# Group A's output squares on GpSimd with one VectorE sum, and group B's outputs scaled for two heads in one operation

## The chip, the cores and the metric

The kernel runs on 1 core of one Trainium2 chip. The metric is the device time of one execution in microseconds. The core has five engines that each work through a queue of instructions in order and wait for one another by semaphores: TensorE (PE in the profile, its weight loads PEld), VectorE (DVE), ScalarE (ACT), GpSimd (POOL) and SyncE (SP), which here issues the DMAs.

## The reference

Two layers of an encoder over 1024 tokens of width 1024, all in float32. What matters here is the attention of the two head groups and what is done to their outputs:

```python
for l in range(DEPTH):                                   # 2 layers
    proj = rms_norm(x, pre_norm_g[l]) @ w_in[l]
    aq, ak, av, ag, bq, bk, bv, bg = jnp.split(proj, SPLIT_POINTS, axis=-1)
    # group A: 4 heads of 128 columns, two softmaxes p[0] - lam * p[1] with a position bias
    oa = diff_attention(aq, ak, av, lam, rel_bias)
    oa = rms_norm(oa, diff_subln_g[l]) * (1.0 - lam_init)       # per head, over its 128 columns
    ya = oa.reshape(bn, s_len, A_WIDTH) * jax.nn.silu(ag)
    # group B: 8 query heads of 64 columns on 2 key heads, q and k normalised and rotated
    ob = gqa_attention(q, k, bv)
    yb = ob * jax.nn.silu(bg)
    y = jnp.concatenate([ya, yb], axis=-1) @ w_out[l]
    x = x + rms_norm(y, post_norm_g[l])
```

`rms_norm(x, g)` is `x * rsqrt(mean(x * x) + 1e-6) * g`. So each row of each of group A's heads needs the sum of 128 squares, and each row of group B's heads needs a division by its softmax sum.

## The kernel before, in words

Tokens are in 8 tiles of 128. Each layer has three stages: the projections, the attention loop, and the output projection. In profiles of this kernel almost every instruction has line 67, that of a helper, so one reads it by tile names: `pS`, `pT`, `pO` are PSUM buffers (two each of scores, transposes and outputs), `e` holds probabilities, `w` split weights or split transposed probabilities, `o` an output on its way to its transpose (2 buffers), `y` the rows that the output projection reads, `s` small per-row numbers.

**The loop.** It goes over 4 heads `h` of group A and, within each, 4 groups `g` of two token tiles: 16 steps a layer. A step takes group A's head `h` and the pair `hp` of group B's heads that goes with it, on 256 tokens. It has 8 items: 4 of group A (two softmaxes for each token tile) and 4 of group B (two heads, two tiles). `tick` handles one item: the row maximum on VectorE (for group A the custom operation that adds the bias as well), the next item's scores on TensorE, one part of an output product, the exponential on ScalarE. Later work is put on lists: `after(n, fn, mid)` runs `fn` n ticks on, in the middle of the tick if `mid`, otherwise at its end; `trans` holds the transposes of probabilities, `parts` the parts of the output products. Within the loop each engine keeps the order in which the code names its instructions (`tc.keep_in_program_order`). So the order on the engines is the order of these lists.

**Group A's output.** `a_out` multiplies values and probabilities into `pO` (transposed: columns of the head by tokens), four parts of 6 matmuls. `finish` copies that to an `o` tile, `oT`. `norm` transposes it back on TensorE into the other half of `pO`, `p4`, and squares it. `gate` copies it into the rows `yv`, and GpSimd works out the factor of each row from the sums of squares `ms` and the reciprocal softmax sums `r0` and scales the rows.

**Group B's output.** `b_out` does the same for two heads, whose values are split in a high and a low half that lie side by side. `finish` copies one half to `oT`; `add`, a tick later, adds the other on VectorE and, for the second head, inverts the softmax sums `sr`; `back` transposes on TensorE at the end of that tick; `store`, one tick later, scales into the rows.

**The tail.** After the last item `tick` goes on while lists are not empty, and the code puts four conversions of output weights (`half_convs`) and the first two transposed row tiles (`y_transposed`, which multiplies with the gates and splits on ScalarE, VectorE and GpSimd) between its ticks. Behind it the output projection begins; there, a scheduler orders the instructions.

Of the kernel before, what the change touches and what calls it, by code (L numbers as in the profile page):

```python
# [11 lines left out]
AF = mybir.ActivationFunctionType  # L12
ALU = mybir.AluOpType
AX = mybir.AxisListType
# [3 lines left out]
P = 128  # L18
# [35 lines left out]
def hybrid_encoder(ctx, tc, x, rel_bias, pre_norm_g, w_in, diff_lambda, diff_subln_g,  # L54
# [18 lines left out]
    pe, dve, act, gps = Engine(nc.tensor), Engine(nc.vector), Engine(nc.scalar), Engine(nc.gpsimd)  # L73
# [11 lines left out]
    def nm(p):  # L85
        uid[0] += 1
        return f"{p}{uid[0]}"
# [10 lines left out]
    def y_tile(shape=(P, D), dt=F32):  # L98
        return sb.tile(list(shape), dt, tag="y", name=nm("y"), bufs=8)

    def o_tile(shape=(P, 512), dt=F32):
        return sb.tile(list(shape), dt, tag="o", name=nm("o"), bufs=2)

    def s_tile(n=1, tag="s", bufs=12):
        return sm.tile([P, n], F32, tag=f"{tag}{n}", name=nm("s"), bufs=bufs)
# [7 lines left out]
    def ps_o():  # L113
        return ps.tile([P, 512], F32, tag="O", name=nm("pO"), bufs=2)
# [189 lines left out]
    def layer(l, hT, ends, given):  # L304
# [14 lines left out]
        def row_tile(t):  # L319
            if ys[t] is None:  # L320
                ys[t] = y_tile()
            return ys[t]
# [435 lines left out]
        def after(delay, fn, mid=False):  # L758
            later_q.append((now[0] + delay, mid, fn))
# [96 lines left out]
        def a_out(h, g, aT, r0):  # L856
            box = []

            def part(i):
                if i == 0:  # L860
                    box.append(ps_o())
                pO = box[0][:, 0:256]
                V = values[h]
                for k in (2 * i, 2 * i + 1):
                    pe.matmul(pO, V[:, 0, k, :], aT[0][:, k, :], start=(k == 0), stop=False)
                    pe.matmul(pO, V[:, 0, k, :], aT[1][:, k, :], start=False, stop=False)
                    pe.matmul(pO, V[:, 1, k, :], aT[0][:, k, :], start=False, stop=(k == NK - 1))
                if i == 3:
                    after(0, lambda: finish(box[0]))

            def finish(pO):
                oT = o_tile((P, 256))
                act.copy(oT, pO[:, 0:256])
                p4 = pO[:, 256:512].rearrange("p (q c) -> p q c", c=P)
                ms = s_tile(2, "oms", 3)
                yv = [row_tile(g * 2 + qi)[:, h * P:(h + 1) * P] for qi in range(2)]

                def norm():
                    for qi in range(2):
                        pe.transpose(p4[:, qi, :], oT[:, qi * P:(qi + 1) * P], ident)  # L880
                    for qi in range(2):
                        act.activation(oT[:, :P], p4[:, qi, :], AF.Square, accum_out=ms[:, qi:qi + 1])
                    after(1, gate, True)

                def gate():
                    for qi in range(2):
                        dve.tensor_copy(yv[qi], p4[:, qi, :])
                    fr = s_tile(2, "ofr", 3)
                    gps.tensor_tensor(fr, r0[:, :2], r0[:, :2], ALU.mult)
                    gps.tensor_tensor(ms, ms, fr, ALU.mult)  # L890
                    gps.tensor_scalar(ms, ms, 1.0 / P, EPS, ALU.mult, ALU.add)
                    gps.tensor_tensor(ms, ms, mhalf[:, :2], ALU.pow)
                    gps.tensor_tensor(fr, ms, r0[:, :2], ALU.mult)
                    for qi in range(2):
                        gps.tensor_scalar(yv[qi], yv[qi], fr[:, qi:qi + 1], 0.0, ALU.mult, ALU.add)
                after(1, norm)

            return [lambda i=i: part(i) for i in range(4)]
# [27 lines left out]
        def b_out(hp, g, BV, bT, sr):  # L926
            kv = hp // 2
            box, halves = [], []

            def part(j, i):  # L930
                if not halves:
                    halves.append(o_tile((P, 256)))
                if i == 0:
                    box.append(ps_o())
                pO = box[j][:, 0:256]
                for k in range(4 * i, 4 * i + 4):
                    pe.matmul(pO, BV[:, kv, k, :], bT[j][0][:, k, :], start=(k == 0), stop=False)
                    pe.matmul(pO, BV[:, kv, k, :], bT[j][1][:, k, :], start=False, stop=(k == NK - 1))
                if i == 1:
                    after(0, lambda: finish(j, box[j], halves[0]))  # L940

            def finish(j, pO, oT):
                mine = slice(j * 64, j * 64 + 64)
                other = slice(64 - j * 64, 128 - j * 64)
                act.copy(oT[mine], pO[other, 0:256])

                def add():
                    dve.tensor_tensor(oT[mine], oT[mine], pO[mine, 0:256], ALU.add)
                    if j == 1:
                        dve.reciprocal(sr, sr)  # L950
                        after(0, back)
                after(1, add, True)
                p4 = pO[:, 256:512].rearrange("p (q c) -> p q c", c=P)

                def back():
                    for qi in range(2):
                        pe.transpose(p4[:, qi, :], oT[:, qi * P:(qi + 1) * P], ident)
                    after(1, store, True)

                def store():  # L960
                    for qi in range(2):
                        for jj in range(2):
                            c0 = 512 + hp * P + jj * 64
                            dve.tensor_scalar(row_tile(g * 2 + qi)[:, c0:c0 + 64], p4[:, qi, jj * 64:jj * 64 + 64],
                                              sr[:, jj * 2 + qi:jj * 2 + qi + 1], None, ALU.mult)

            return [[lambda j=j, i=i: part(j, i) for i in range(2)] for j in range(2)]

# [277 lines left out]
```

## Time and profile before

| | |
|---|---|
| runs | 1414.98, 1415.23, 1417.01 us; median 1415.23 |
| the profiled execution | 1416.01 us, its span 1414.3 us |
| granted TensorE clock | 0.997 on average |
| busy share of the span | VectorE 73%, ScalarE 59%, GpSimd 51% |
| attention loops with their tails | about 305 to 617 us and 1003 to 1317 us |

The profiled execution's own time is 1.7 us longer than its span, from the first to the last instruction. A row of the timeline gives the start in us from the span's start, the length in us, the engine, the line, the operation, the tiles (out<-in) with their shapes, how many instructions are merged, and in brackets how long the engine had been idle and what ended that.

### The profile page before, as it was taken

The numbers are of one execution on the slowest core, as the hardware profiler recorded it, in microseconds if no ns is written. First come the engines' busy times: TensorE is split into PE (matmuls) and PEld (weight loads), VectorE is DVE, ScalarE is ACT, GpSimd is POOL, SyncE is SP. The second block draws the span as 40 slices with busy tenths as digits, with TensorE's granted clock in tenths as the row PEclk, the third lists the DMA queues.
The fourth block names the chain that finished last, engine by engine and source line by source line (L and its number), as shares of the span: only waits on it lengthen the run. The fifth ranks groups of instructions, "written<-read, shape, count | busy, mean of one in ns | idle before, by whom it ended". The sixth has DMA issues, their size and how long they took to land.

```text
span 1414.3 us, 22659 instructions
## 1 busy us (share of the span) xinstructions
PE 1385.7 (98%) x8108; PEld 1214.0 (86%) x8108; DVE 1033.3 (73%) x1737; ACT 832.1 (59%) x1586; POOL 724.2 (51%) x827
## 2 busy tenths in 40 slices
PE   7999999999999999999999999999999999999998
PEld 6888888889999999978788888888899999999787
DVE  7879854478888888852787797554788888888423
ACT  6323443378888888843442143333888888888321
POOL 5530000068888888874343200001888888888641
PEclk9999999999999999999999999999999999999999
DMA  6456436583514232143524455337823151222313
GB/s 225 125 154 188 161 133 224 165 247 91 126 53 111 68 98 90 46 134 119 180 93 122 128 155 178 119 112 225 217 70 87 53 155 53 71 87 84 125 61 134
DMA packets 134784, 179.12 MB, mean 127 GB/s; under 512 B 10112, under 2 KB 98432, under 8 KB 132368
## 3 DMA queue, kind: packets, MB, share of 16 engines
q1 hardware_dynamic: 134672, 177.67, 41.6%
q8 instruction: 64, 1.05, 0.3%
q14 instruction: 48, 0.39, 0.1%
HBM read 120.98 MB, written 60.85 MB: 129 GB/s over the span
## 4 chain that ended last, share of the span: by engine, by line
PE 91%; POOL 3%; DVE 2%; DMA 2%; ACT 1%; issue 1%; POOLq 0%; DVEq 0%; SPq 0%; ACTq 0%
PE pO L67 38%; PE pS L67 32%; PE pT L67 21%; POOL w L67 1%; DVE y L67 1%; DMA h<-aq_d 1%; POOL e L67 1%; ACT e L67 1%; POOL h L67 0%; DVE w L67 0%; DMA e<-in_pre_norm_g_dram 0%; DVE h L67 0%; DVE s L67 0%; DMA e<-x_d 0%; ACT w L67 0%
## 5 line engine op out<-in xcount | busy, mean ns | idle before, releaser
L67 PE MATMUL pO<-w,h 128*128 128x256 f32 (+1 forms) x3160 | 551.0, 322 | 2.6 <-POOL w L67 2.6
L67 PEld LDWEIGHTS pO<-w,h 128*128 128x128 f32 x3160 | 486.1, 189 | 67.2 <-POOL w L67 3.6
L67 PE MATMUL pS<-h,h 128*128 128x512 f32 x1024 | 293.6, 409 | 0.6 <-DMA h<-aq_d 0.5
L67 POOL TENSOR_TENSOR y<-y,y 128x512 fp32r<-128x512 f32 x12 | 15.5, 1292 | 382.2 <-ACT y L67 192.6
L67 PE MATMUL pT<-identr,e 128*128 128x128 f32 x1536 | 200.5, 273 | 0.5
L67 PEld LDWEIGHTS pS<-h,h 128*128 128x128 f32 x1024 | 174.9, 189 | 24.4 <-ACT w L67 0.7
L67 DVE TENSOR_TENSOR w<-pT,w 128x512 fp32r<-128x512 f32 x256 | 169.9, 685 | 35.4 <-ACT w L67 35.2
L67 PEld LDWEIGHTS pT<-identr,e 128*128 128x128 f32 x1536 | 172.5, 140 | 5.2 <-DVE w L67 4.2
L67 POOL TENSOR_TENSOR w<-e,w 128x512 fp32r<-128x512 f32 x128 | 166.2, 1299 | 10.4
L67 ACT CAST w<-pT 128x512 fp32r<-128x512 f32 x256 | 143.9, 588 | 40.8 <-PE pT L67 38.0
L67 DVE TENSOR_REDUCE s<-pS 128x1 f32<-128x1024 f32 x128 | 156.4, 1222 | 15.0 <-PE pS L67 14.1
L67 DVE CUSTOM_DVE_ANT_0 e<-pS,h 128x1024 f32<-128x1024 f32 x128 | 155.6, 1217 | 6.7 <-PE pS L67 6.1
L67 ACT ACTIVATE e<-e,s 128x1024 f32<-128x1024 f32 x128 | 148.2, 1158 | 19.5 <-DVE s L67 18.8
L67 POOL TENSOR_TENSOR e<-e,e 128x1024 f32<-128x1024 f32 x64 | 153.3, 2395 | 5.3
L67 ACT ACTIVATE e<-pS,s 128x1024 f32<-128x1024 f32 x128 | 144.6, 1130 | 5.6 <-DVE s L67 5.2
L67 PE MATMUL pT<-h,w 128*128 128x512 f32 x528 | 122.5, 389 | 0.0
L67 PE MATMUL pS<-w,h 128*128 128x512 f32 (+1 forms) x576 | 118.0, 362 | 0.0
L67 PEld LDWEIGHTS pT<-h,w 128*128 128x128 f32 x528 | 99.0, 188 | 20.9 <-ACT w L67 0.2
L67 PEld LDWEIGHTS pS<-w,h 128*128 128x128 f32 x576 | 96.6, 194 | 14.6
L67 POOL TENSOR_SCALAR e<-e,s 128x1024 f32<-128x1024 f32 x64 | 72.0, 1126 | 72.0 <-DVE s L67 68.3
L67 ACT ACTIVATE o<-pO 128x128 f32<-128x128 f32 (+3 forms) x101 | 39.4, 390 | 108.6 <-PE pO L67 107.4
L67 POOL TENSOR_TENSOR s<-s,mhalf 128x2 f32<-128x2 f32 (+2 forms) x96 | 80.0, 834 | 8.0
(102 smaller groups left out, 1794.2 us busy)
## 6 DMA issues: line engine op xcount, KB each, us to landing
h<-aq_d SPq DMA_DIRECT2D x64, 256.0 KB, 5.1
h<-in_w_in_dram SPq DMA_DIRECT2D x20, 512.0 KB, 4.7
bq_d<-y SPq DMA_DIRECT2D x64, 128.0 KB, 2.4
av_d<-e SPq DMA_DIRECT2D x32, 256.0 KB, 2.3
e<-in_w_in_dram SPq DMA_DIRECT2D x16, 512.0 KB, 4.7
y<-in_w_in_dram SPq DMA_DIRECT2D x16, 512.0 KB, 6.3
ak_d<-e SPq DMA_DIRECT2D x32, 256.0 KB, 2.0
gate_d<-e SPq DMA_DIRECT2D x32, 256.0 KB, 2.0
```

Of the source, the lines that this page charges most:

```text
L67: ins = fn(*args, **kw)
```

## The change

Group A: ScalarE no longer squares the transposed output out of PSUM. GpSimd squares the copies in `yv` (SBUF) into `oT`, whose content has been transposed by then; one VectorE operation sums both tiles' squares into `ms`. That sum and the small operations of the scale, which followed the copies directly, stand in a new function `scale`, one tick after `gate`.

Group B: the four VectorE operations that scale 64 columns each by one number a row become two of 128 columns, whose factor is a view of `sr` repeated over 64 columns.

```diff
                 def norm():
                     for qi in range(2):
                         pe.transpose(p4[:, qi, :], oT[:, qi * P:(qi + 1) * P], ident)
-                    for qi in range(2):
-                        act.activation(oT[:, :P], p4[:, qi, :], AF.Square, accum_out=ms[:, qi:qi + 1])
                     after(1, gate, True)
 
                 def gate():
                     for qi in range(2):
                         dve.tensor_copy(yv[qi], p4[:, qi, :])
+                    for qi in range(2):
+                        gps.tensor_tensor(oT[:, qi * P:qi * P + P], yv[qi], yv[qi], ALU.mult)
+                    after(1, scale, True)
+
+                def scale():
+                    dve.tensor_reduce(out=ms, in_=oT.rearrange("p (q c) -> p q c", c=P), axis=AX.X, op=ALU.add)
                     fr = s_tile(2, "ofr", 3)
                     gps.tensor_tensor(fr, r0[:, :2], r0[:, :2], ALU.mult)
                     gps.tensor_tensor(ms, ms, fr, ALU.mult)
...
                 def store():
                     for qi in range(2):
-                        for jj in range(2):
-                            c0 = 512 + hp * P + jj * 64
-                            dve.tensor_scalar(row_tile(g * 2 + qi)[:, c0:c0 + 64], p4[:, qi, jj * 64:jj * 64 + 64],
-                                              sr[:, jj * 2 + qi:jj * 2 + qi + 1], None, ALU.mult)
+                        c0 = 512 + hp * P
+                        two = lambda v: v.rearrange("p (j c) -> p j c", j=2)
+                        dve.tensor_tensor(two(row_tile(g * 2 + qi)[:, c0:c0 + P]), two(p4[:, qi, :]),
+                                          sr[:, qi::2].rearrange("p (j o) -> p j o", o=1).broadcast_to([P, 2, 64]),
+                                          ALU.mult)
```

In the loop TensorE's and SyncE's instructions keep their order. What moves stands on VectorE and GpSimd. VectorE in one step of layer 0 (the copies of `gate` are COPY, the bias sum is ISA, group B's `add` is o<-o,pO, followed by the reciprocal of `sr`), before:

```order
L67 COPY y_2920<-pO_3927 128x128
L67 COPY y_2921<-pO_3927 128x128
L67 TENSOR_TENSOR w_3970<-pT_4069,w_3969 128x4x128
L67 ISA e_4114,s_4115<-pS_4094,h_2658 128x1024
L67 ISA s_4115 128x1
L67 TENSOR_TENSOR o_3852<-o_3852,pO_4051 64x256
L67 RECIPROCAL s_3484<-s_3484 128x4
L67 TENSOR_REDUCE s_4149<-pS_4119 128x1
L67 TENSOR_SCALAR y_2920<-pO_4051,s_3484 128x64 x2
L67 TENSOR_SCALAR y_2921<-pO_4051,s_3484 128x64 x2
```

and after:

```order
L67 COPY y_2920<-pO_3923 128x128
L67 COPY y_2921<-pO_3923 128x128
L67 TENSOR_TENSOR w_3966<-pT_4063,w_3965 128x4x128
L67 ISA e_4102,s_4103<-pS_4082,h_2658 128x1024
L67 ISA s_4103 128x1
L67 TENSOR_REDUCE s_4018<-o_4016 128x2
L67 TENSOR_TENSOR o_3850<-o_3850,pO_4047 64x256
L67 RECIPROCAL s_3482<-s_3482 128x4
L67 TENSOR_REDUCE s_4146<-pS_4116 128x1
L67 TENSOR_TENSOR y_2920<-pO_4047,s_3482 128x128
L67 TENSOR_TENSOR y_2921<-pO_4047,s_3482 128x128
```

The sum of squares (s_4018<-o_4016) stands ahead of group B's sum, and the four scalings are two. GpSimd in the same step (w<-e is the split of a tile of transposed probabilities, e<-e the difference of group A's two softmaxes, s<-s the factor of the scale), before:

```order
L67 CAST w_3840<-e_3934 128x4x128
L67 TENSOR_TENSOR w_3841<-e_3934,w_3840 128x4x128
L67 TENSOR_TENSOR s_4086<-s_3483 128x2
L67 TENSOR_TENSOR s_4022<-s_4022,s_4086 128x2
L67 TENSOR_SCALAR s_4022<-s_4022 128x2
L67 TENSOR_TENSOR s_4022<-s_4022,mhalf 128x2
L67 TENSOR_TENSOR s_4086<-s_4022,s_3483 128x2
L67 TENSOR_SCALAR y_2920<-y_2920,s_4086 128x128
L67 TENSOR_SCALAR y_2921<-y_2921,s_4086 128x128
L67 CAST w_3969<-e_4011 128x4x128
L67 TENSOR_TENSOR w_3970<-e_4011,w_3969 128x4x128
```

and after:

```order
L67 CAST w_3829<-e_3930 128x4x128
L67 TENSOR_TENSOR w_3830<-e_3930,w_3829 128x4x128
L67 TENSOR_TENSOR o_4016<-y_2920 128x128
L67 TENSOR_TENSOR o_4016<-y_2921 128x128
L67 CAST w_3965<-e_4007 128x4x128
L67 TENSOR_TENSOR w_3966<-e_4007,w_3965 128x4x128
L67 TENSOR_TENSOR s_4106<-s_3481 128x2
L67 TENSOR_TENSOR s_4018<-s_4018,s_4106 128x2
L67 TENSOR_SCALAR s_4018<-s_4018 128x2
L67 TENSOR_TENSOR s_4018<-s_4018,mhalf 128x2
L67 TENSOR_TENSOR s_4106<-s_4018,s_3481 128x2
L67 TENSOR_SCALAR y_2920<-y_2920,s_4106 128x128
```

The squares stand where the scale began, and the scale has moved behind the next split. GpSimd in the tail of layer 0 (h<-h is `y_transposed`'s split, w<-h the conversion of output weights), before:

```order
L67 TENSOR_TENSOR w_6858<-h_6482,w_6857 128x1024
L67 CAST w_6704<-e_6781 128x4x128
L67 TENSOR_TENSOR w_6705<-e_6781,w_6704 128x4x128
L67 TENSOR_TENSOR w_6914<-h_6485,w_6913 128x1024
L67 TENSOR_TENSOR s_6972<-s_6492 128x2
L67 TENSOR_TENSOR h_7003<-h_6824,h_7003 128x512
L67 TENSOR_TENSOR s_6956<-s_6956,s_6972 128x2
```

and after:

```order
L67 TENSOR_TENSOR w_6845<-h_6469,w_6844 128x1024
L67 CAST w_6690<-e_6767 128x4x128
L67 TENSOR_TENSOR w_6691<-e_6767,w_6690 128x4x128
L67 TENSOR_TENSOR w_6899<-h_6472,w_6898 128x1024
L67 TENSOR_TENSOR h_6987<-h_6802,h_6987 128x512
L67 TENSOR_TENSOR o_6939<-y_3746 128x128
L67 TENSOR_TENSOR o_6939<-y_3747 128x128
L67 TENSOR_TENSOR s_6967<-s_6479 128x2
```

The last step's squares stand behind the split of 128x512. TensorE at the end of the tail of layer 0 (pO<-identr,o are group B's last transposes back, of `back`; pT<-identr,y those of `y_transposed`), before:

```order
L67 MATMUL pT_7051<-identr,y_3195 128x128 x2
L67 MATMUL pT_7058<-identr,y_3195 128x128 x4
L67 MATMUL pO_7020<-w_6857,h_6826 128x512
L67 MATMUL pO_7020<-w_6858,h_6826 128x512
L67 MATMUL pO_6957<-identr,o_6845 128x128 x2
L67 MATMUL pO_7020<-w_6857,h_6826 128x512 x2
```

and after:

```order
L67 MATMUL pT_7035<-identr,y_3194 128x128 x2
L67 MATMUL pO_7004<-w_6844,h_6804 128x512
L67 MATMUL pO_7004<-w_6845,h_6804 128x512
L67 MATMUL pO_7004<-w_6844,h_6804 128x512 x2
L67 MATMUL pO_7004<-w_6845,h_6804 128x512
L67 MATMUL pO_7004<-w_6844,h_6804 128x512 x2
L67 MATMUL pO_6942<-identr,o_6832 128x128 x2
```

The transposes back stand behind seven products of the output projection instead of two, and four of `y_transposed`'s transposes have moved behind all 24 products of the first tile.

## The prediction

> **What bounds the kernel now.** I read the page's busy times first, then the windows, the waits, and last the timeline of one step. TensorE is busy for nearly the whole span:
>
> ```profile
> PE 1385.7 (98%) x8108; PEld 1214.0 (86%) x8108; DVE 1033.3 (73%) x1737; ACT 832.1 (59%) x1586; POOL 724.2 (51%) x827
> ```
>
> An average over stages says little. The windows give the attention loop of layer 0 alone, and the stretch in which it runs out (the tail) in both layers:
>
> ```profile
> core 0: us, PE busy (x) PEld busy (x) DVE busy (x) ACT busy (x) POOL busy (x), PEclk, DMA share, GB/s
> 330.00:590.00 260.00, 260.00 (x1844) 241.69 (x1843) 226.66 (x438) 227.60 (x462) 218.84 (x251) 1.00 0.29 82
> 600.00:615.00 15.00, 13.25 (x107) 11.97 (x105) 11.28 (x20) 11.41 (x23) 14.40 (x15) 1.00 0.43 141
> 615.00:620.00 5.00, 3.39 (x19) 3.12 (x20) 4.70 (x9) 2.49 (x8) 4.92 (x4) 0.82 0.28 92
> 1310.00:1320.00 10.00, 8.31 (x56) 7.14 (x55) 9.07 (x17) 4.94 (x12) 9.74 (x9) 1.00 0.37 113
> ```
>
> In the loop TensorE has 260.00 of 260 us, at full clock; VectorE, ScalarE and GpSimd have 84 to 88%. So relief of ScalarE cannot shorten the loop, while any wait that reaches TensorE lengthens it at once and is never made good. In the tail it is GpSimd that is full (14.40 of 15 us, 4.92 of 5), and TensorE that has holes.
>
> The waits of the same loop window contain none of TensorE, and one that the change takes away: group A's copies on VectorE wait for ScalarE's squares, 13 times in 260 us, once for each step.
>
> ```profile
> DVE y L67 <- ACT o L67: 10.4, 13, 0.8
> ```
>
> One step, from the timeline (start, us, engine, what, and the idle time before it):
>
> ```profile
> 400.87 1.13 POOL L67 TENSOR_SCALAR e<-e,s 128x1024 f32<-128x1024 f32 x1 [1.96 <-DVE s L67]
> ...
> 404.10 1.17 PE L67 MATMUL pS<-h,h 128*128 128x512 f32 x4
> ...
> 404.37 0.49 DVE L67 COPY y<-pO 128x128 f32<-128x128 f32 x2 [0.80 <-ACT o L67]
> ...
> 405.11 1.31 POOL L67 TENSOR_TENSOR w<-e,w 128x512 fp32r<-128x512 f32 x1
> ...
> 405.45 1.21 DVE L67 CUSTOM_DVE_ANT_0 e<-pS,h 128x1024 f32<-128x1024 f32 x1
> ...
> 406.37 0.20 POOL L67 TENSOR_TENSOR s<-s 128x2 f32<-128x2 f32 x1
> ...
> 406.86 0.42 DVE L67 TENSOR_TENSOR o<-o,pO 64x256 f32<-64x256 f32 x1 [0.18 <-ACT o L67]
> ...
> 407.83 0.25 PEld L67 LDWEIGHTS pO<-identr,o 128*128 128x128 f32 x2
> ...
> 408.67 0.85 DVE L67 TENSOR_SCALAR y<-pO,s 128x64 f32<-128x64 f32 x4
> 409.43 1.28 DVE L67 TENSOR_TENSOR w<-pT,w 128x512 fp32r<-128x512 f32 x2
> ...
> 410.92 1.03 PE L67 MATMUL pT<-identr,e 128*128 128x128 f32 x8
> ...
> 411.21 1.12 POOL L67 TENSOR_SCALAR e<-e,s 128x1024 f32<-128x1024 f32 x1 [0.26 <-DVE s L67]
> ...
> 412.42 2.40 POOL L67 TENSOR_TENSOR e<-e,e 128x1024 f32<-128x1024 f32 x1
> ...
> 415.54 1.22 DVE L67 CUSTOM_DVE_ANT_0 e<-pS,h 128x1024 f32<-128x1024 f32 x1 [0.16 <-PE pS L67]
> ...
> 420.62 1.14 POOL L67 TENSOR_SCALAR e<-e,s 128x1024 f32<-128x1024 f32 x1 [1.96 <-DVE s L67]
> ```
>
> The first and the last row are the same operation of two neighbouring steps: a step is 19.75 us, and GpSimd idles 1.96 us ahead of each, so nothing of its lag is carried over. The reader is to see one thing above all: group B's sum on VectorE (o<-o,pO, 406.86 to 407.28) ends only 0.55 us before TensorE loads it for the transposes back (407.83). That is the slack into which the change puts a new operation.
>
> **The change part by part.** Prices of what is new, from the groups by shape (count, busy us, mean ns):
>
> ```profile
> L67 POOL TENSOR_TENSOR y<-y,y 128x512 fp32r<-128x512 f32 x12 | 15.5, 1292 | 382.2 <-ACT y L67 192.6 <-DMA h<-rep_d 185.1 <-DMA aq_d<-y 4.4
> ...
> L67 POOL TENSOR_TENSOR e<-e,e 128x1024 f32<-128x1024 f32 x64 | 153.3, 2395 | 5.3
> ...
> L67 DVE TENSOR_REDUCE s<-e 128x8 f32<-128x512 f32 x16 | 11.0, 685 | 18.7 <-ACT e L67 18.6
> ...
> L67 DVE TENSOR_REDUCE s<-e 128x2 f32<-128x128 f32 x16 | 4.5, 282 | 5.0 <-ACT e L67 4.9
> ...
> L67 DVE TENSOR_TENSOR y<-pT,y 128x128 fp32r<-128x128 f32 x16 | 4.4, 285 | 1.2 <-ACT y L67 1.0
> ...
> L67 ACT ACTIVATE o<-pO 128x128 f32<-128x128 f32 x64 | 17.8, 278 | 13.0 <-PE pO L67 11.9
> ```
>
> *Squares off ScalarE:* 64 of 278 ns with their accumulator reads. ScalarE waits for others at 87% load and stands on no path of the loop, so this is worth nothing there. Nor is the copies' lost wait of 0.8 us: they start 0.8 earlier, but the bias sum behind them, at 405.45, still needs the scores that TensorE ends at 405.27.
>
> *Squares on GpSimd:* a 128x128 product has no row. Between 512 and 1024 columns a column costs (2395 - 1292)/512 = 2.15 ns, the rest is 189 ns; at 128 columns 465 ns. Two take 0.93, or 0.91 with the small overlap of neighbours. They stand where the small operations of the scale stood, so they start when the product of 405.11 ends, at 406.37, and end at 407.28.
>
> *The sum on VectorE:* (685 - 282)/384 = 1.05 ns a column, so 0.42 us for 256. VectorE is free at 406.66 but the sum must wait for GpSimd until about 407.33 (0.05 to pass the semaphore; the tail's rows below show 0.06 from VectorE to TensorE). In the queue it stands **ahead** of group B's sum, of the reciprocal, of the next row maximum and, through these, of TensorE's transposes back and ScalarE's next exponential. It ends at 407.75; group B's sum follows with about 0.05 overlap, 407.70 to 408.12; TensorE can load at 408.18 instead of 407.83. **TensorE waits 0.35 us in each step.** Since every engine follows TensorE, the next step repeats it. From both sides: if squares cost only the fixed part (two times 0.19), the sum ends 0.53 earlier and the wait is 0; if GpSimd is slowed as its pair of 128x512 products in the tail is (1.75 us each, below, against 1.29), the squares take 1.26 and the wait is 0.70. I take 0.35, since the loop's own GpSimd products are at 1.30. There are 16 steps a layer, of which 14 end inside the loop: 28 x 0.35 = 9.8 us.
>
> *What is late next in the step:* VectorE is then 0.84 behind its old times and TensorE 0.35. The two scalings (below) give back 0.28, so the pair of subtractions of 409.43 ends at about 411.3, and TensorE, which overwrites the second of their banks half-way through the transposes of 410.92 + 0.35, comes at 411.8: hidden. GpSimd does the cast and product of the next tile first and the scale last. Its own new time is 0.91 less the 0.26 of idle ahead of 411.21, so its queue is 0.65 later at the product of 412.42, which then ends at 415.47; the bias sum of 415.54, which overwrites a tile that this product reads, comes at 415.89: hidden. The scale itself feeds only rows that are read after the loop.
>
> *Group B's four scalings become two:* from 0.85 to about 2 x 0.285 = 0.57 us on VectorE, on no path: worth 0 by itself, and counted above as catching up. Without that cover the subtractions would be 0.28 later, still within the 0.5 left.
>
> *DMAs:* none is added, and SyncE's queue has the same rows.
>
> *The tail.* GpSimd is full there, and TensorE waits for it:
>
> ```profile
> 604.45 0.42 DVE L67 TENSOR_TENSOR o<-o,pO 64x256 f32<-64x256 f32 x1
> ...
> 604.93 0.44 PE L67 MATMUL pO<-identr,o 128*128 128x128 f32 x2 [0.51 <-DVE o L67]
> ...
> 608.38 3.50 POOL L67 TENSOR_TENSOR h<-h,h 128x512 fp32r<-128x512 f32 x2
> ...
> 617.40 2.81 POOL L67 TENSOR_TENSOR w<-h,w 128x1024 fp32r<-128x1024 f32 x1
> 617.49 1.29 PE L67 MATMUL pO<-w,h 128*128 128x256 f32 x7 [1.28 <-POOL w L67]
> ...
> 620.32 1.27 POOL L67 TENSOR_TENSOR h<-h,h 128x512 fp32r<-128x512 f32 x1
> ...
> 631.83 1.03 PE L67 MATMUL pT<-identr,y 128*128 128x128 f32 x8
> ...
> 1315.08 2.85 POOL L67 TENSOR_TENSOR w<-h,w 128x1024 fp32r<-128x1024 f32 x1
> 1315.17 1.09 PE L67 MATMUL pO<-w,h 128*128 128x256 f32 x7 [1.29 <-POOL w L67]
> ...
> 1316.11 0.88 PE L67 MATMUL pT<-identr,y 128*128 128x128 f32 x6
> ...
> 1317.43 10.69 PE L67 MATMUL pO<-w,h 128*128 128x512 f32 x46
> ...
> 1327.96 1.03 PE L67 MATMUL pT<-identr,y 128*128 128x128 f32 x8
> ```
>
> First, the squares of the last step but one lengthen GpSimd's unbroken queue by 0.93, so TensorE's waits at 617.49 and 1315.17 end 0.93 later. (The same step's transposes back, at 604.93, are late too, but TensorE has that time before it meets the GpSimd wait.) Second, the last step's squares stand behind the 128x1024 product and a 128x512 one, and TensorE needs group B's sum behind them. Layer 1: GpSimd 1315.08 + 0.93 + 2.85 + 1.27 + 0.91 = 1321.04; the semaphore, the sum and group B's sum (0.05 + 0.42 + 0.37 + 0.06) make 1321.94. TensorE comes there after the eight products (1.09), two transposes (0.29) and seven 128x512 products (7 x 0.232): 1315.17 + 0.93 + 3.01 = 1319.11. It waits 2.8 us. Layer 0 likewise, at its lower clock, 2.4 us. Together 2 x 0.93 + 2.8 + 2.4 = **7.1 us**. The ends: 0, if the list of what stands ahead of the squares clears early, and 9 with both waits 1 us longer. ScalarE's relief saves nothing here, since GpSimd is the one waited for.
>
> **Sum.** 9.8 + 7.1 = 16.9 us on the profiled execution's 1416.0 us (span 1414.3) gives 1432.9. That execution lies 0.8 above the median of the runs, 1415.23, so the median to expect is 1432.
>
> **A rule weighed.** With the row first: around TensorE's wait of 1.28 us the granted clock falls to 0.82 (615 to 620), and around the equal wait of layer 1 it stays at 1.00. From the end of the wait to the next transposes the first takes 631.83 - 617.49 = 14.34 us, the second 12.79, so one drop costs 1.55 us. The Trainium skill ("TensorE: Matmul & The Clock Gate", the section on the HAM clock gate) says that the clock halves after at least one idle window of about 3.4 us. By that rule waits of 2.4 to 2.8 us drop nothing and the sum stays 1432; by the rows a shorter wait has done it, and a drop in layer 1 as well would make 1433.6. I leave it out of the sum and in the range.
>
> **The rivals.**
> 1. *The loop hides it, the tail doesn't.* The squares would have to end by 406.93, 0.35 earlier, against 465 ns from two rows of the same operation. 1415.2 + 7.1 = 1422.
> 2. *The squares are slowed,* as GpSimd's products are at 608.38 while VectorE works there too: wait 0.70 a step, 19.6 + 9 = 28.6, so 1444. Against it: in the loop VectorE finishes its bias sum 0.3 us after the squares start and then waits for them.
> 3. *Nothing is seen.* The operations leave ScalarE, and all new waits fall into slack: 1415. It needs rival 1's condition and a tail without cost.
> 4. *Faster.* If the ends of matmuls, which are modelled, hid that the period of 19.75 us is set by the ring of ScalarE and VectorE, then the 0.8 us wait that goes would shorten it. From 0.1 us a step it would beat 0.2%; with 0.3, 8.4 us go and the time is 1407. Against it: 260.00 of 260 us, and no wait of TensorE in that window.
>
> **How the numbers follow.** The forecast 64%; rival 1 13%; rival 2 10%; rival 3 7%; rival 4 6%. The forecast's own bounds are waits of 0.2 to 0.5 a step and 5 to 9 us in the tails: 1426 to 1438. The range 1421 to 1441 takes in rival 1 and part of rival 2. 0.2% is 2.8 us, about what a measurement of this kernel can tell from no change: faster 6%, same 7%, slower 87%.
>
> **What would show it.** Right: in the loop a wait of TensorE for VectorE's o, about 0.35 us and 14 times a layer, ahead of the transposes back; a wait of VectorE's sum for GpSimd's o of about 0.7 us; a step of 20.1 us; GpSimd products of about 465 ns; in each tail one TensorE wait of 2 to 3 us for VectorE's o. No wait of VectorE's copies for ScalarE. Wrong: a step of 19.75 us still (rival 1 or 3), a shorter one (4), or squares over 0.6 us (2).

## The result and the profile after

The changed kernel takes 1429.05 us (median of 5 runs, 1428.36 to 1430.84), the kernel before 1415.79 (1414.98 to 1417.01): ratio 1.0103, 95% interval 1.0092 to 1.0115. (The two medians alone give 1.0094, at the low end of that interval; the ratios in this text are those on record, and can differ from the quotient of the medians beside them.) The profiled execution has a span of 1427.3 us against 1414.3, so 13.0 us more.

The page's busy times, then the windows (us, PE busy, PEld, DVE, ACT, POOL, granted clock, DMA share, GB/s) of the changed kernel:

```profile
PE 1392.5 (98%) x8108; PEld 1213.5 (85%) x8108; DVE 1032.4 (72%) x1705; ACT 811.7 (57%) x1458; POOL 745.6 (52%) x891
```

```profile
330.00:590.00 260.00, 259.99 (x1824) 239.16 (x1823) 225.66 (x420) 217.18 (x406) 225.09 (x276) 1.00 0.28 82
...
625.00:630.00 5.00, 4.00 (x12) 3.18 (x13) 2.17 (x6) 0.62 (x1) 4.28 (x10) 0.66 0.93 305
...
1325.00:1330.00 5.00, 2.72 (x14) 1.98 (x13) 1.52 (x4) 0.98 (x2) 4.38 (x8) 0.96 0.90 263
1330.00:1335.00 5.00, 5.00 (x17) 3.96 (x16) 0.65 (x3) 0.62 (x1) 3.57 (x6) 0.70 0.76 264
```

In the loop's window ScalarE has 10.4 us less to do (227.60 before) and GpSimd 6.3 more. TensorE is still at 260 of 260 us, but it gets 1824 matmuls through in that time where it got 1844: the busy time doesn't show the loss, the count does. (Over the whole span both traces hold the same 8108 matmuls, so no missing records make this difference.) The waits of the same window name its cause (in all, times, longest):

```profile
DVE s L67 <- POOL o L67: 6.6, 13, 0.5
...
PEld pO L67 <- DVE o L67: 2.5, 13, 0.2
```

VectorE's sum waits for GpSimd's squares once in each step, and TensorE's weight load for group B's sum, once in each step. One step in the timeline:

```profile
406.75 0.76 POOL L67 TENSOR_TENSOR o<-y 128x128 f32<-128x128 f32 x2
...
407.54 0.42 DVE L67 TENSOR_REDUCE s<-o 128x2 f32<-128x256 f32 x1 [0.50 <-POOL o L67]
407.99 0.42 DVE L67 TENSOR_TENSOR o<-o,pO 64x256 f32<-64x256 f32 x1
408.47 0.20 PEld L67 LDWEIGHTS pO<-identr,o 128*128 128x128 f32 x2 [0.19 <-DVE o L67]
...
426.69 0.76 POOL L67 TENSOR_TENSOR o<-y 128x128 f32<-128x128 f32 x2
```

Read downwards, the four operations stand end to end: squares, sum, group B's sum, weight load, with 0.03 to 0.06 us between them. The last row is the next step's squares: a step is 19.94 us (19.75 before). In the tail of layer 0 TensorE waits twice in that chain (at 607.88 and 626.00), once for GpSimd's split weights (at 620.79), and VectorE's sum waits once for long:

```profile
607.88 0.44 PE L67 MATMUL pO<-identr,o 128*128 128x128 f32 x2 [1.84 <-DVE o L67]
...
620.79 1.10 PE L67 MATMUL pO<-w,h 128*128 128x256 f32 x7 [1.28 <-POOL w L67]
...
624.28 0.75 POOL L67 TENSOR_TENSOR o<-y 128x128 f32<-128x128 f32 x2
...
625.07 0.42 DVE L67 TENSOR_REDUCE s<-o 128x2 f32<-128x256 f32 x1 [4.45 <-POOL o L67]
...
626.00 0.44 PE L67 MATMUL pO<-identr,o 128*128 128x128 f32 x2 [2.25 <-DVE o L67]
```

Where the 13.0 us lie is seen by setting group B's transposes back of each step beside those of the kernel before (start of their weight load, after less before; worked out from both traces):

| place (time before) | after less before, us | gained since |
|---|---|---|
| first step of layer 0 (328.8) | -0.18 | |
| 14th step of layer 0 (585.6) | +2.35 | 13 x 0.195 |
| first step of layer 1 (1026.5) | +5.40 | tail of layer 0, and one more step |
| 14th step of layer 1 (1283.3) | +7.96 | 13 x 0.197 |
| end of the span | +13.0 | tail of layer 1 |

With one step's share taken to the loop each time, the loops lose 5.5 us, the tails 2.9 and 5.0, and the execution began 0.4 ahead.

### The profile page after: what moved, and what is told of

Read it like the earlier page. It is cut to its first block, busy times and chain, and to the rows that moved or that the text cites. A ratio compares the mean times of both kernels' runs of the same rounds, so it can differ in the third digit from the quotient of the medians.

```text
span 1427.3 us, 22559 instructions
## 1 busy us (share of the span) xinstructions
PE 1392.5 (98%) x8108; PEld 1213.5 (85%) x8108; DVE 1032.4 (72%) x1705; ACT 811.7 (57%) x1458; POOL 745.6 (52%) x891
## 3 DMA queue, kind: packets, MB, share of 16 engines
q8 instruction: 64, 1.05, 0.3%
## 4 chain that ended last, share of the span: by engine, by line
PE 91%; DVE 3%; POOL 2%; ACT 2%; issue 1%; DMA 0%; DVEq 0%; POOLq 0%; SPq 0%; ACTq 0%
PE pO L67 38%; PE pS L67 31%; PE pT L67 21%; DVE y L67 1%; POOL e L67 1%; POOL w L67 1%; DVE h L67 1%; ACT w L67 1%; ACT e L67 1%; DVE s L67 1%; DMA e<-in_pre_norm_g_dram 0%; DVE w L67 0%; POOL s L67 0%; POOL o L67 0%; ACT h L67 0%
## 5 line engine op out<-in xcount | busy, mean ns | idle before, releaser
L67 POOL TENSOR_SCALAR s<-s 128x2 f32<-128x2 f32 (+2 forms) x96 | 22.1, 230 | 114.7 <-DVE s L67 72.4
```

The costliest lines, as they stand in the source:

```text
L67: ins = fn(*args, **kw)
```

## The experiments

The theory: VectorE works in order, the change put a sum that waits for GpSimd in front of group B's sum, and TensorE, the bound of the loop, waits for that one. The rivals: the load on GpSimd itself (C), the length of the sum on VectorE (D), group B's edit (A), and for the tails a lag that the loop brings in (F).

**The two parts alone.** First group B's edit alone, the kernel before with

```diff
-                        for jj in range(2):
-                            dve.tensor_scalar(row_tile(...)[:, c0:c0 + 64], p4[:, qi, jj * 64:...], sr[...], None, ALU.mult)
+                        dve.tensor_tensor(two(row_tile(g * 2 + qi)[:, c0:c0 + P]), two(p4[:, qi, :]), ..., ALU.mult)
```

> The kernel before with group B's edit alone: two scalings of two heads each, squares still on ScalarE. Theory (the loss comes from VectorE's new sum, which waits for GpSimd's squares in front of group B's sum): this edit shortens VectorE's queue by 0.28 us at a place off the path, so no change, 1415.8 us within 1 us, and no wait of TensorE for VectorE's o in the loop. Rival A (the scalings with a broadcast operand carry part of the loss): up to 1421. Rival B (relief of VectorE is worth something by itself): 28 steps x 0.28 us would give 1408.

Measured 1415.09 us, the kernel before 1415.09 on the same chip; ratio 1.000 (0.999 to 1.001). In 330:590 VectorE has 222.81 us of work instead of 226.66, and nothing follows from it. Then group A's edit alone, the changed kernel with that hunk undone:

> The kernel after with group A's edit alone: squares on GpSimd, one sum on VectorE, and group B's four scalings as before. Theory: the whole loss is here, 1429 us, at most 1431 where the 0.28 us that the two wider scalings gave back was used. Rival A (part of the loss is group B's): clearly below 1429, 1421 to 1426.

Measured 1431.15 us, ratio 1.0117 (1.0102 to 1.0131), 0.15 above the end of the range. The whole loss is group A's. The step loses 0.23 us here against 0.195 with both edits (mean of 13 steps), so beside group A's edit the wider scalings are worth about 0.04 us a step. The prediction had them at nothing (still within the 0.5 left); by which path they count isn't shown.

**The place of the sum.** The changed kernel with one line changed, so that the sum stands behind group B's sum:

```diff
-                    after(1, scale, True)
+                    after(1, scale)
```

> The kernel after, with VectorE's sum of group A's squares put at the end of its stage instead of the middle: it stands behind group B's sum and the reciprocal, in front of the next row maximum. GpSimd's squares, their number and their place in GpSimd's queue stay. Theory (the place in VectorE's queue): TensorE's 13 waits of 0.19 us in 330:590 go, and so do both waits for VectorE's o in each tail except the 0.5 us that the kernel before had; left are some 0.8 us a tail from GpSimd's longer queue: 1415.8 + 1.6 = 1417.4 us, from 1416 to 1419. Rival C (the loss is GpSimd's added load of 0.76 us a step, wherever the sum stands): still 1429. Rival D (the sum's own 0.42 us on VectorE, wherever it stands): the loop keeps 5.3 us, 1421 or more.

Measured 1417.81 us, ratio 1.0021 (1.0011 to 1.0031). The step in its timeline, and the loop's window:

```profile
406.60 0.76 POOL L67 TENSOR_TENSOR o<-y 128x128 f32<-128x128 f32 x2
...
406.89 0.42 DVE L67 TENSOR_TENSOR o<-o,pO 64x256 f32<-64x256 f32 x1
...
407.44 0.39 DVE L67 TENSOR_REDUCE s<-o 128x2 f32<-128x256 f32 x1
```

```profile
330.00:590.00 260.00, 260.00 (x1845) 241.73 (x1844) 227.38 (x424) 219.57 (x409) 227.84 (x282) 1.00 0.29 82
```

Group B's sum now runs beside GpSimd's squares and the new sum behind it, with no wait. The same work, and more GpSimd work in the window than in the changed kernel (227.84 us against 225.09), gives 1845 matmuls: rivals C and D fall for the loop. The transposes back keep one distance to those of the kernel before, +0.22 us in layer 0's loop and +0.25 in layer 1's. What is left of the loss lies in the tails, where TensorE now waits 1.11 us for GpSimd's w (at 616.73 and 1314.45).

**More of the suspected wait.** The changed kernel with a third product on GpSimd:

```diff
                         gps.tensor_tensor(oT[:, qi * P:qi * P + P], yv[qi], yv[qi], ALU.mult)
+                    gps.tensor_tensor(oT[:, :P], yv[0], yv[0], ALU.mult)
```

> The kernel after with a third product on GpSimd behind the two squares (the first square once more, so the result is the same): 0.38 us more in front of the sum. Theory: the wait of TensorE in each loop step goes from 0.19 to 0.57 us, 28 x 0.38 = 10.6 us; in the tails 0.4 to 0.8 each, together 1429 + 12 = 1441 us; VectorE's wait for GpSimd's o goes from 0.50 to 0.88 us a step. Rival C (GpSimd's load in general, which has 35 us idle in 330:590): nothing in the loop until that idle time is used, 1429 to 1431.

Measured 1441.85 us, ratio 1.0184 (1.0170 to 1.0197).

```profile
410.09 1.12 POOL L67 TENSOR_TENSOR o<-y 128x128 f32<-128x128 f32 x3
411.24 0.42 DVE L67 TENSOR_REDUCE s<-o 128x2 f32<-128x256 f32 x1 [0.89 <-POOL o L67]
411.70 0.42 DVE L67 TENSOR_TENSOR o<-o,pO 64x256 f32<-64x256 f32 x1
412.17 0.20 PEld L67 LDWEIGHTS pO<-identr,o 128*128 128x128 f32 x2 [0.58 <-DVE o L67]
```

0.36 us more in the squares, 0.39 more in VectorE's wait, 0.39 more in TensorE's, and 0.575 us lost in each step: each link passes its delay on to the next undiminished.

**The same sum without the wait.** The kernel before, with a sum of 256 columns that nobody reads, at the same place:

```diff
+                def dummy():
+                    dve.tensor_reduce(out=s_tile(2, "dum", 3), in_=oT.rearrange("p (q c) -> p q c", c=P), axis=AX.X, op=ALU.add)
...
                         dve.tensor_copy(yv[qi], p4[:, qi, :])
+                    after(1, dummy, True)
```

> The kernel before, with one more sum of 256 columns on VectorE whose result nobody reads, at the very place where the change puts its sum (in front of group B's sum, one for each step). The squares stay on ScalarE, so it waits for nobody. Theory (it is the wait for GpSimd that costs, not the sum's length): the sum runs from 406.7 to 407.1 us of the step, where VectorE was idle or had slack; group B's sum ends 0.2 us later and still 0.3 us before TensorE loads it: no change in the loop, 1415 to 1416.5 us in all. Rival D (the sum's 0.42 us in VectorE's queue is the cost): 0.2 to 0.42 us a step, 1421 to 1427.

Measured 1420.79 us, ratio 1.0047 (1.0035 to 1.0059): as a time, a miss of the theory, and only 0.2 us below rival D's range. The trace tells the two apart. The transposes back stay at -0.41 us to the kernel before in 13 steps of layer 0's loop and at +0.21 in layer 1's, so the loop loses nothing; the tails do. VectorE's and then GpSimd's timeline of the first tail:

```profile
610.62 0.67 DVE L67 TENSOR_TENSOR w<-pT,w 128x512 fp32r<-128x512 f32 x1
611.58 3.36 DVE L67 TENSOR_TENSOR w<-h,w 128x1024 fp32r<-128x1024 f32 x1 [0.29 <-POOL h L67]
```

```profile
608.00 3.51 POOL L67 TENSOR_TENSOR h<-h,h 128x512 fp32r<-128x512 f32 x2
611.47 2.39 POOL L67 TENSOR_TENSOR w<-h,w 128x1024 fp32r<-128x1024 f32 x1
```

VectorE's difference of 128x1024 took 3.36 us beside GpSimd's, which had begun 0.11 earlier; the like one of the kernel before, at 611.68, took 1.28. TensorE then waits 1.98 us for VectorE's h (at 615.66; 0.40 before). To test where the loss lies, the unread sum was left out of the last two steps of each layer (`if not (h == 3 and g >= 2)` ahead of it):

> The kernel before with the unread sum of 256 columns on VectorE (as in the run before) in the first 14 steps of each layer alone, not in the last two. That run came out 6 us slower, but its transposes back keep one distance to those of the kernel before through the whole loop (-0.41 us at all of 13 steps in layer 0, +0.21 in layer 1), and leave it in the tails. Theory (without a wait for GpSimd the sum costs the loop nothing; the tails lost because VectorE's and GpSimd's long products met otherwise there): no change, 1414.8 us, within 1 us. Rival D (the sum's length costs in the loop): 1418 or more.

Measured 1414.79 us against 1415.23, ratio 1.0001 (0.9992 to 1.001). So the sum's own 0.42 us cost the loop nothing, and what it cost lay in the last two steps.

**Loop and tails apart.** Group A's old form in the last two steps of each layer, the new one elsewhere (group B's edit stays everywhere; the code in outline):

```diff
+                if h == 3 and g >= 2:
+                    (norm and gate of before)
+                else:
+                    (norm, gate and scale of after)
```

> The kernel after, with the old form (squares on ScalarE, no sum) in the last two of the 16 steps of each layer. Theory: the loop's part alone is left, 0.195 us for 27 to 28 steps = 5.4 us, and the tails are those of the kernel before: 1415.1 + 5.4 = 1420.5 us, from 1419.5 to 1422; TensorE's waits for VectorE's o in the tails are 0.5 us each, two in all. Rival E (the loop's lag is absorbed by the holes of the tails, and the tails' loss is the real one): 1416 to 1418. Rival F (the tails' loss is a lag that the loop brings in, not GpSimd's queue there): still 1426 to 1428.

Measured 1420.57 us, ratio 1.0043 (1.0030 to 1.0056), with the step's loss of 0.195 us and two waits for VectorE's o of 0.5 us. And the reverse, the new form in the last two steps alone:

> The counterpart of the run with the old form in the last two steps: here only these two steps of each layer have the new form, and the 14 steps of the loop have the old one. Theory (loop and tails add up): the loop keeps its step of 19.75 us, and the tails' part is left, the changed kernel's 13 to 14.5 us less the loop's 5.5, so 7.5 to 9 us: 1423 to 1424, with the two waits of TensorE for VectorE's o of about 1.8 and 2.3 us in each tail. Rival F (the tails' waits come from the lag that the loop brings in): 1416 to 1419.

Measured 1423.88 us against 1414.55, ratio 1.0062 (1.0048 to 1.0076); its loop keeps one distance to the kernel before in all 13 steps. The two waits stand in layer 0 as told (1.85 and 2.25 us). In layer 1 of the profiled execution, the slowest of the five, the first is there (1.84) but the second is not: the clock fell early (0.73 and 0.93 from 1305 to 1315), and behind it TensorE waits 1.51 us for VectorE's h and 2.79 for its y. The two parts, 0.43% and 0.62%, add up to 1.05% where the whole change costs 1.03%, each known to within about 0.13. Rivals E and F fall: the tails lose about as much with no lag brought in.

**The relief without the wait.** The late sum in the loop, the old form in the last two steps, group B's edit everywhere:

> The change as it might have been: squares on GpSimd in the first 14 steps of each layer, VectorE's sum behind group B's sum, the old form in the last two steps, group B's two scalings everywhere. ScalarE has 10 us less work in 330:590 than in the kernel before, GpSimd 8 more. Theory (TensorE is the bound, and neither the relief nor the load reaches it): no change, 1414.8 us, within 1 us, with a step of 19.75 us. Rival C (GpSimd's load costs something in the loop): 1418 or more. Rival G (relief of ScalarE has a value once the new wait is gone): below 1412.

Measured 1415.20 us against 1415.23, ratio 0.9998 (0.9989 to 1.0007). ScalarE has 219.55 us of work in 330:590 instead of 227.60, GpSimd 227.84 instead of 218.84, and the time is the old one. So rivals C and G fall too. This is the best form of the change that was found, and it is worth nothing.

**The size of a square.** The product of two different row tiles in place of each square:

```diff
-                        gps.tensor_tensor(oT[:, qi * P:qi * P + P], yv[qi], yv[qi], ALU.mult)
+                        gps.tensor_tensor(oT[:, qi * P:qi * P + P], yv[qi], yv[1 - qi], ALU.mult)
...
-                    gps.tensor_tensor(ms, ms, fr, ALU.mult)
+                    gps.tensor_tensor(ms, ms, ms, ALU.mult)
```

> The kernel after, with each square replaced by the product of two different tiles (row tile 1 times row tile 2), and the sums squared where they were multiplied by the reciprocals' square, so that the normalization of group A is another one. It asks why a square took 399 ns where 465 had been worked out. If two different inputs cost GpSimd more than one input read twice: 440 to 470 ns each and some 0.1 us more wait in front of VectorE's sum (0.60 instead of 0.50 a step), 1431. If the working was at fault (a straight line through 512 and 1024 columns does not hold at 128): 399 ns still, 1428 to 1429.

Measured 1431.43 us, one execution. The groups by shape (count, busy us, mean ns), of this kernel and of the changed one:

```profile
L67 POOL TENSOR_TENSOR o<-y,y 128x128 f32<-128x128 f32 x64 | 28.1, 459 | 0.0
```

```profile
L67 POOL TENSOR_TENSOR o<-y 128x128 f32<-128x128 f32 x64 | 24.2, 399 | 0.0
```

Two inputs cost 459 ns, one input read twice 399. With 459 the step lost 0.32 us.

**Two tries at the tails.** Both leave the change out and aim at TensorE's wait of 1.28 us for GpSimd. In the first, VectorE splits the last two probability tiles of group B in place of GpSimd (`pool_half` is None for h, g, j of 3, 3, 1):

> The kernel before, with the second half of group B's last two probability tiles of each layer split by VectorE (0.64 us each, straight from PSUM) in place of GpSimd (a cast of 0.61 and a difference of 1.28 us each). Nothing of the change is in it. Theory (in the tails GpSimd's queue is what TensorE waits for): the wait of 1.28 us for GpSimd's w goes in both layers, and with it the 1.5 us of lower clock in layer 0: 1412 us, from 1410.5 to 1414. Rival (VectorE, busy 4.70 of 5 us there, becomes the one that is late): 1415 to 1417.

Measured 1417.77 us, ratio 1.0021 (1.0012 to 1.0031): the theory missed, and the rival's direction came true, a little beyond its range. The waits for GpSimd's w are gone, but in both tails TensorE now waits 2.51 us for VectorE's w, where VectorE's difference of 128x1024 took 3.52 us (2.06 before, at 608.69):

```profile
608.68 3.52 DVE L67 TENSOR_TENSOR w<-h,w 128x1024 fp32r<-128x1024 f32 x1 [0.87 <-issue]
...
613.18 1.44 PE L67 MATMUL pT<-identr,y 128*128 128x128 f32 x8 [2.51 <-DVE w L67]
```

In the second, `ENDING = (3, 2, 3, 4, 0, 5)` in place of `(1, 2, 3, 4, 0, 5)`:

> The kernel before with one number of the tails' order changed: the first half of the output weights is converted two steps later, so that on GpSimd its difference of 128x1024 (3.38 us) stands behind the last probability tile's cast and difference, for which TensorE waits 1.28 us in each tail, and no longer in front. No work is added or taken. Theory (in the tails GpSimd's queue is what TensorE waits for): the two waits go, 2.6 us, and with them the drop of the clock of 1.7 us in layer 0: 1410.5 to 1413. Rival (VectorE, which has the next half's difference behind GpSimd's, or its products when they run beside GpSimd's, gets late instead): 1415 to 1418.

Measured 1421.95 us, ratio 1.0052 (1.0039 to 1.0065): the theory missed again, and the loss is 4 us larger than the rival allowed. The wait for GpSimd is gone here too, and TensorE waits for VectorE's h instead:

```profile
615.62 1.25 PE L67 MATMUL pT<-identr,y 128*128 128x128 f32 x8 [1.54 <-DVE h L67]
...
621.11 0.95 PE L67 MATMUL pT<-identr,y 128*128 128x128 f32 x4 [2.16 <-DVE h L67]
```

VectorE's, then GpSimd's rows ahead of those waits:

```profile
612.60 2.31 DVE L67 TENSOR_TENSOR w<-h,w 128x1024 fp32r<-128x1024 f32 x1 [0.90 <-POOL w L67]
...
616.98 3.47 DVE L67 TENSOR_TENSOR h<-h,h 128x512 fp32r<-128x512 f32 x2
```

```profile
613.78 6.12 POOL L67 TENSOR_TENSOR w<-h,w 128x1024 fp32r<-128x1024 f32 x2
```

In both, one wait was traded for a longer one. No version that was run beats the kernel before.

## Why the prediction was right, and where its sizes were off

*The mechanism of the loop: right.* The chain of squares, sum, group B's sum and weight load is in the timeline as told, and three runs show it to be the cause: it goes when the sum stands later, it grows with a third product, and the sum without its wait costs the loop nothing.

*The size of the loop's wait: too large.* The step that failed is "Two take 0.93, or 0.91": the pair took 0.76 us. The line through 512 and 1024 columns, 465 ns, was drawn through products of two inputs, and for those it holds (459 measured). A square reads one. With 0.76 in place of 0.91 the forecast's wait of 0.35 becomes 0.20; 0.19 was measured. The loop's term of 9.8 us was 5.5. The sum (0.42 forecast, 420 ns measured) and group B's scaling (285 and 281 ns) were right.

*Where the wait shows: partly.* It stands under the weight loads (PEld), and TensorE's own row stays at 259.99 of 260 us. Who looks for it in TensorE's busy time finds nothing.

*The tails' waits: right, in part by luck.* For the waits at 617.49 and 1315.17, "end 0.93 later" was forecast; the first ends at 620.79, of which 2.35 us came in from the loop, so 0.95 later. In layer 1 it is 1324.10 - 1315.17 - 7.96 = 0.97. But the reason given, the squares' 0.93 in GpSimd's queue, brought 0.76 of that. The rest is what else changed in that queue, the same in both tails: its pair of 128x512 products took 2.53 us instead of 3.50, one small operation of the scale (128x2) 1.03 instead of 0.19, and a cast 1.08 instead of 0.61. The three come to about +0.3 together, which the prediction had not counted. The waits of the last step, forecast at 2.4 and 2.8, are 2.25 and 2.28 us; in layer 1 GpSimd's product of 128x1024 ahead of it took 2.39 us where 2.85 was counted. The wait of 1.84 us at 607.88 (0.51 before) is swallowed by the wait for GpSimd behind it, as was said. Together 6.45 us against 7.1.

*The clock: left out of the sum, and it came, by chance.* In the prediction a drop of the clock in layer 1 stood outside the sum. In the profiled execution it happened: 1325 to 1335 ran at 0.96 and 0.70, which is 5 x (0.04 + 0.30) = 1.7 us, as much as layer 0's 5 x (1 - 0.66) after and its 0.82 of before with the slice behind it (kernel before):

```profile
620.00:625.00 5.00, 5.00 (x21) 4.03 (x20) 2.09 (x6) 1.24 (x2) 4.65 (x10) 0.84 0.97 312
```

So layer 0 lost 1.7 us before and after, and layer 1 after alone. This is the rule that the prediction weighed: by the Trainium skill ("TensorE: Matmul & The Clock Gate", the section on the HAM clock gate) it takes an idle window of about 3.4 us, but the longest single wait ahead of these drops was 2.28 us, and the row was the better guide. It is no certain loss, though, and not one of the change alone. The run with the unread sum in the loop alone has the tails of the kernel before, and its profiled execution shows no drop from 605 to 630 us and a span of 1411.5. The run with the old form in the last two steps has those tails as well, and shows 0.66 in both (620 to 625 and 1320 to 1325). So whether a tail loses these 1.7 us differs between executions, and what decides it stays open.

*The sum of it.* Loop 5.5 and tails 6.45, the clock 1.7, less the 0.4 of the start, make 13.2 against 13.0 in the spans. The forecast of 16.9 had 4.3 too much in the loop, 0.65 too much in the tails' waits and 1.7 too little in the clock, so part of its closeness is that errors point against each other, and one of them, the clock, is chance.

*The rivals.* Rival 1 (the loop hides it) needed the squares done by 406.93, 0.35 earlier than forecast; the pair came 0.15 earlier and the wait stayed. Rival 2 (slowed squares) and rival 3 (nothing) didn't occur. Rival 4 (relief of ScalarE makes it faster) was put to the test by itself: 0.9998.

## What to carry to other kernels

What an operation costs on a busy in-order engine is set less by its length than by what stands behind it: ask of each new operation what it waits for, and who waits for the operation behind it. Here 0.42 us on VectorE cost nothing, and the same 0.42 us behind a wait for another engine cost the bound engine 0.19 us in each step; one line that put it behind the critical sum took the loop's loss away. Relief of an engine that the bound engine doesn't wait for can be worth nothing: here 8 us less on ScalarE in 260 changed nothing. And where the bound engine reads as 100% busy, count its instructions in a fixed window rather than its busy time.

## What the runs showed of the hardware

A GpSimd product of 128x128 float32 takes 399 ns when both inputs are one tile, and 459 with two tiles.

VectorE's and GpSimd's long products, when both read two tiles of SBUF, slow each other in these tails, and the rows read as if one waited for the other to end. VectorE's pair of 128x512 differences took 1.72 us in the changed kernel (at 617.89), 2.79 in the kernel before (615.19) and 3.47 with the other order of the tail (616.98), where one of them took 0.69 us while GpSimd stood still (616.84, VectorE's split); its difference of 128x1024 took 1.24 to 3.52. In the row of 3.36 us above, GpSimd's operation ended 2.28 us after VectorE's began, and 1.08 us were left, somewhat less than the operation takes alone; the operation ahead of it that reads PSUM (w<-pT,w) kept its 0.67 us during GpSimd's 3.51. With the new form in the last two steps alone, VectorE's at 1314.03 began 0.92 us behind GpSimd's and again ended 1.08 us after it. In the kernel before, VectorE's began first, by 0.16 us, and there it is GpSimd's that took longer, 3.38 us where the like one of the changed kernel took 2.38 (at 620.70):

```profile
611.68 1.28 DVE L67 TENSOR_TENSOR w<-h,w 128x1024 fp32r<-128x1024 f32 x1
...
611.84 3.38 POOL L67 TENSOR_TENSOR w<-h,w 128x1024 fp32r<-128x1024 f32 x1
```

The Trainium skill ("SBUF — State Buffer", section "SBUF: two separate sides") calls the port pair that the two engines share an exclusive lock, held for a whole instruction, which VectorE needs, against a GpSimd operation that reads SBUF, when both of its own inputs lie in SBUF; the traces agree (3.36 us and 3.38 us for the one that began second). It would explain why the tails answered to small shifts with 3 to 7 us, and why both tries to relieve GpSimd there failed; that reading of the tails is argued from the rows and wasn't tested by an experiment that takes the contention alone away.
